# An encoder trunk on one core: three attentions of half B beside its q and k, and half B's last output projection two FFN steps earlier, in token sets of three and two with an FFN step behind every token tile

## The chip, the cores and the metric

The kernel runs on one core of a Trainium2 chip. The metric is the device time of one execution in microseconds (us); the time before is the median of three runs. Engines are called as the profile calls them: PE (TensorE matmul), PEld (its weight loads), DVE (VectorE), ACT (ScalarE), POOL (GpSimd), SP (SyncE, which issues most DMAs).

## The reference, cut to what matters

A trunk of two layers on 1024 prompt frames and 64 frames of a running stream, all in float32. Layer 0 mixes with RWKV-7 and gated linear attention, layer 1 with attention over a band of chunks; behind each mixing there is an output projection, a layer norm, a SwiGLU channel mixer (FFN) and another layer norm. The change touches layer 1:

```python
def chunk_band_attention(x, w_qkv, rel_table, w_o, cache_k, cache_v):
    qkv = (x @ w_qkv).reshape(Bsz, T, 3, C_HEADS, C_HEAD_DIM)
    q, k, v = (jnp.swapaxes(qkv[:, :, i], 1, 2) for i in range(3))
    o = ...          # softmax(q k / 8 + bias) v over a frame's own chunk and the 8 before it, 16 heads
    y = jnp.swapaxes(o, 1, 2).reshape(Bsz, T, D_MODEL) @ w_o
    return y, k_rows, v_rows
...
        x = layer_norm(DEEPNORM_ALPHA * x + mix, P['ln1_w'][layer], P['ln1_b'][layer])
        x = layer_norm(DEEPNORM_ALPHA * x + swiglu(x, P['ffn_w_in'][layer], P['ffn_w_out'][layer]),
                       P['ln2_w'][layer], P['ln2_b'][layer])
```

D_MODEL is 1024, there are 16 heads of 64, and the FFN's hidden width is 2816, which is 22 tiles of 128.

## The kernel before, in words

**Halves.** The tokens are split in half A (index 0: 384 prompt and the 64 sample frames, 448 columns) and half B (index 1: 640 prompt frames, five tiles of 128). The halves go through the same stages at different times, so that one half's vector work lies beside the other half's matmuls. Each float32 product is made of three fp32r products (high x high, low x high, high x low); a weight tile is loaded by `load_w` (L92) into one of two raw buffers `wr`, cast to `wh` on ACT (L101), and its rest `wl` is made on DVE (L106), on POOL (L108), or by both.

**The end of the program.** In `run`, half B's q and k are made for eight pairs of heads by `qk(1, hp)`; after the pairs listed in `self.AQ` (L1343) one attention of half B is queued there. An attention is queued in parts: score matmuls (L1283, L1284), softmax on DVE, ACT, DVE and POOL (L1287 to L1294), transposes on PE (L1299), casts on ACT and DVE (L1309, L1310), and the product with v (L1325, "PV"). Its result goes through DRAM (`og_d`). The other attentions lie in the loop at L1472 beside half A's FFN of layer 1, `f = self.ffn(0, 1, ...)` (L917), a generator of 22 steps: each `next(f)` is one step of 48 matmuls of 448 columns (L124 to L126), and behind the steps in GROUPS (16, 18 and 22 among them) comes a group of the second FFN matrix through `tsg` (L135 to L138 with `hh`, `hl`). When the loop at L1476 has done step `self.JM`, half B's last output projection is set up: its operand is loaded from `og_d` and cast (`load_xt`, L205 to L216, `yraw`), the residual x is loaded from `x_d` (`load_acc`, L797), one more `next(f)` runs, and `proj` (L851) goes through the token tiles in the order 2, 0, 3, 1, 4, in sets of which each loads all of `w_o`. `tsg` (L801) multiplies a tile (`part`, 12 matmuls of 512 columns), adds it to `acc` (L827), and behind a tile's last part calls `between` (another piece of `f`) and `after` (the layer norm).

**The layer norm** (L869) is a chain across three engines: L883 and L885 on DVE, L887 and L888 on POOL (`rstd`), L891 on DVE, then for the left half L893 on ACT and L894 on POOL and for the right half L896 on DVE, then eight transposes on PE (L901).

**Behind it** half B's last FFN runs as `s_ffn` (L1049), in products of fewer matmuls that need sums of the normed tokens (`chunk`, L966 to L1011, whose low halves L114 are put by POOL: eight `put` for each tile) and sums of the weights (`s_weights`, L1020: loads L1028, casts L1034 and L1035, four sums on POOL, L1040 to L1045). Half A's last layer norm `ln2` lies beside its first steps. The scheduler of the framework decides the order on each engine from the order in which the work is written and what each piece waits for.

Of the kernel before, what the change touches and what calls it, by code (L numbers as in the profile page):

```python
# [83 lines left out]
class Kern:  # L84
# [715 lines left out]
    def tsg(self, hf, acc, wsrc, pairs, hi, lo, first, after=None, packed=None, between=None, toks=None):  # L800

        def load(nh):
            ws = []
            for pr in pairs:
                h_, l_ = self.load_w(wsrc(nh, pr), [128, 2, 512])
                ws += [(h_[:, j, :], l_[:, j, :]) for j in range(2)]  # L810
            return ws

        kts = [2 * pr + j for pr in pairs for j in range(2)]
        toks = toks or self.toks(hf)

        def part(ws, nh, i, t0, m):
            two = packed and m == 64
            ps = self.bank()
            if two:
                self.gemm_ts(ps, ws, packed, None, kts, lambda x: x[:, 0:128])  # L820
            else:
                self.gemm_ts(ps[:m], ws, hi, lo, kts, lambda x: x[:, t0 : t0 + m])
            a = acc[i][:m, 512 * nh : 512 * nh + 512]
            if first:
                self.V.scalar_tensor_tensor(a, a, ALPHA, ps[:m], op0=ALU.mult, op1=ALU.add)
            else:
                self.V.tensor_tensor(a, a, ps[:m], op=ALU.add)  # L827
            if two:
                self.V.tensor_tensor(a, a, ps[m:], op=ALU.add)

        if after is None or between:
            for nh in range(2):
                ws = load(nh)
                for i, t0, m in toks:
                    part(ws, nh, i, t0, m)
                    if after and nh:
                        if between is not True:
                            between(i)
                        after(i)
        else:  # L840
            ws = [load(nh) for nh in range(2)]
            for i, t0, m in toks:
                for nh in range(2):
                    part(ws[nh], nh, i, t0, m)
                after(i)
# [491 lines left out]
    def run(self):  # L1337
# [2 lines left out]
        self.wkv_d = self.dp.tile([4, 128, 64], F32, name="wkv_d", tag="wkv_d")  # L1340
        self.gla_d = self.dp.tile([2, 128, 128], F32, name="gla_d", tag="gla_d")
        self.JX = 2
        self.PB, self.QB, self.turn, self.AQ = 1, 2, 0, (2, 5)  # L1343
        self.HB, self.PRE, self.JO, self.JM = 5, 4, 16, 18
        es_scan, es_one, es_ps = ExitStack(), ExitStack(), ExitStack()
        self.sp_ps = es_ps.enter_context(tc.tile_pool(name="scps", bufs=1, space=PS))
        self.tpsum = lambda: self.sbank("tps")
# [75 lines left out]
        with tc.tile_pool(name="qp", bufs=1) as qp:  # L1423
            self.vproj(0, qp, 2)
            for hp in range(4):
                if hp == self.JX:
                    with tc.tile_pool(name="yr1", bufs=1, side="right") as yp:
                        self.load_xt(1, self.yg_d, (4, 5, 6, 7, 0, 1, 2, 3), pool=yp)
                    acc1 = self.load_acc(1, a["x"], accp)
# [12 lines left out]
        f = self.ffn(1, 0, acc1, hp, lambda: self.layer_norm(1, acc1, "ln2", 0, xd(1)))  # L1442
# [11 lines left out]
        with tc.tile_pool(name="at1", bufs=1, side="right") as atp:  # L1454
# [16 lines left out]
            f = self.ffn(0, 1, acc0, hp, lambda: later.append, True)  # L1471
# [5 lines left out]
        for j in f:  # L1477
            if j == self.JM:
                self.gp2 = self.ctx.enter_context(tc.tile_pool(name="gp2", bufs=1, space=PS))
                self.tpsum = self.bank  # L1480
                accp = self.ctx.enter_context(tc.tile_pool(name="accB1", bufs=1, side="right"))
                self.xt[1] = self.xt_tiles(xbp, 1)
                with tc.tile_pool(name="yr2", bufs=1, side="right") as yp, tc.issue_after(self.last_w):
                    self.load_xt(1, self.og_d, pool=yp)
                    self.paired = True
                    acc1 = self.load_acc(1, self.x_d, accp)
                xs, sums = self.s_operands(self.ctx.enter_context(tc.tile_pool(name="sx", bufs=1, side="right")),
                                           self.ctx.enter_context(tc.tile_pool(name="st", bufs=1, side="right")))
                next(f)
                self.proj(1, acc1, "w_o", self.layer_norm(1, acc1, "ln1", 1, sums=sums), between=lambda i: next(f) if i in (3, 1, 4) else None, first=2)  # L1490
        es_a.close()
        hp = self.ctx.enter_context(tc.tile_pool(name="hpB1", bufs=1))
        outB = lambda t0, m: a["y_p"][PA + t0 : PA + t0 + m, :]
# [95 lines left out]
```

## Time and profile before

| | |
|---|---|
| median of 3 runs | 3117.12 us (3116.71 to 3119.89) |
| the profiled execution's own time | 3121.6 us |
| its span, first to last instruction | 3119.8 us |
| PE busy | 3017.0 us, 97% of the span |
| DVE, ACT, POOL busy | 2021.3, 1272.0, 1363.5 us |
| mean granted TensorE clock | 0.975 |

The page gives for each engine how long it was busy; the views below it give, for a stretch of the program, what an engine waited for. Times in the timeline count from the span's start. A matmul's own time there is longer than the distance from its start to the next one's, since matmuls overlap; costs are counted from start to start. The granted clock is 1.00 at 2.4 GHz and 0.50 at 1.2 GHz, the two levels that it has.

### The profile page before, as it was taken

The numbers are of one execution on the slowest core, as the hardware profiler recorded it, in microseconds if no ns is written. First come the engines' busy times: TensorE is split into PE (matmuls) and PEld (weight loads), VectorE is DVE, ScalarE is ACT, GpSimd is POOL, SyncE is SP. The second block draws the span as 40 slices with busy tenths as digits, with TensorE's granted clock in tenths as the row PEclk, the third lists the DMA queues.
The fourth block names the chain that finished last, engine by engine and source line by source line (L and its number), as shares of the span: only waits on it lengthen the run. The fifth ranks groups of instructions, "written<-read, shape, count | busy, mean of one in ns | idle before, by whom it ended". The sixth has DMA issues, their size and how long they took to land. (4 is left out here: it accounts for less than half of the span.)

```text
span 3119.8 us, 50045 instructions
## 1 busy us (share of the span) xinstructions
PE 3017.0 (97%) x17468; PEld 2676.2 (86%) x17468; DVE 2021.3 (65%) x4941; ACT 1272.0 (41%) x2761; POOL 1363.5 (44%) x1489
## 2 busy tenths in 40 slices
PE   9999999899999999999999999999999989899998
PEld 7788888688888887888999899899999978799987
DVE  4677875879898764455554466245666667766567
ACT  4454554344454323233443132345444433333332
POOL 2354534444454333443332233244555555745444
PEclk9989999889999999999999999999999999999999
DMA  6554334533533228444343232866455443322222
GB/s 201 140 155 119 108 109 123 141 105 109 137 110 112 89 97 274 140 134 123 116 133 105 81 95 98 247 201 182 126 150 145 132 160 107 116 80 95 67 82 75
DMA packets 298492, 399.29 MB, mean 128 GB/s; under 512 B 125504, under 2 KB 218552, under 8 KB 298240
## 3 DMA queue, kind: packets, MB, share of 16 engines
q1 hardware_dynamic: 297088, 393.48, 42.4%
q8 instruction: 138, 2.26, 0.3%
q10 hardware_dynamic: 1152, 2.62, 0.2%
q14 instruction: 114, 0.93, 0.1%
HBM read 323.63 MB, written 75.51 MB: 128 GB/s over the span
## 5 line engine op out<-in xcount | busy, mean ns | idle before, releaser
L108 POOL TENSOR_TENSOR wl<-wr,wh 128x512 fp32r<-128x512 f32 (+2 forms) x297 | 521.7, 1760 | 642.1 <-ACT wh L101 592.3
L124 PE MATMUL gps<-xh,wh 128*128 128x320 f32 (+1 forms) x2188 | 746.0, 341 | 7.8 <-ACT xh L215 5.9
L125 PE MATMUL gps<-xl,wh 128*128 128x320 f32 (+1 forms) x2188 | 745.0, 340 | 0.6 <-DVE xl L216 0.6
L126 PE MATMUL gps<-xh,wl 128*128 128x320 f32 (+1 forms) x2188 | 744.3, 340 | 0.9 <-DVE wl L106 0.9
L101 ACT CAST wh<-wr 128x1024 fp32r<-128x1024 f32 x360 | 375.8, 1048 | 457.3 <-PE gps L125 131.2
L106 DVE TENSOR_TENSOR wl<-wr,wh 128x512 fp32r<-128x512 f32 (+2 forms) x297 | 289.6, 975 | 248.9 <-ACT wh L101 246.0
L124 PEld LDWEIGHTS gps<-xh,wh 128*128 128x128 f32 x2188 | 414.4, 189 | 30.6 <-ACT xh L215 5.9
L126 PEld LDWEIGHTS gps<-xh,wl 128*128 128x128 f32 x2188 | 413.8, 189 | 19.9 <-DVE wl L106 2.1
L125 PEld LDWEIGHTS gps<-xl,wh 128*128 128x128 f32 x2188 | 414.0, 189 | 18.1 <-DVE xl L216 1.0
L1294 POOL TENSOR_SCALAR s<-s,mx 128x640 f32<-128x640 f32 (+5 forms) x144 | 203.9, 1416 | 272.1 <-DVE mx L1293 250.7
L135 PE MATMUL gps<-wh,xh 128*128 128x512 f32 x661 | 262.0, 403 | 6.8 <-ACT xh L1092 2.5
L138 PE MATMUL gps<-wh,xl 128*128 128x512 f32 x661 | 258.9, 399 | 6.1 <-DVE xl L216 6.1
L136 PE MATMUL gps<-wl,xh 128*128 128x512 f32 x661 | 263.0, 400 | 1.3 <-DVE wl L106 1.1
L136 PE MATMUL gps<-wl,hh 128*128 128x512 f32 x572 | 226.7, 398 | 0.3 <-DVE wl L106 0.3
L135 PE MATMUL gps<-wh,hh 128*128 128x512 f32 x572 | 226.2, 397 | 0.3 <-DVE acc L827 0.3
L827 DVE TENSOR_TENSOR acc<-acc,gps 128x512 f32<-128x512 f32 x216 | 143.6, 679 | 86.8 <-PE gps L138 83.6
L138 PE MATMUL gps<-wh,hl 128*128 128x512 f32 x484 | 189.5, 398 | 2.2 <-DVE hl L942 2.2
L549 DVE TENSOR_TENSOR t<-lt,x 16x48 f32<-16x48 f32 (+9 forms) x540 | 147.3, 273 | 35.8 <-DMA lt<-l_d 25.4
L1292 ACT ACTIVATE s<-s,mx 128x640 f32<-128x640 f32 (+5 forms) x144 | 96.4, 669 | 162.3 <-DVE mx L1291 153.8
L135 PEld LDWEIGHTS gps<-wh,xh 128*128 128x128 f32 x661 | 125.9, 191 | 37.6 <-ACT wh L101 4.3
L138 PEld LDWEIGHTS gps<-wh,xl 128*128 128x128 f32 x661 | 125.7, 190 | 34.4 <-DVE xl L216 6.9
L136 PEld LDWEIGHTS gps<-wl,xh 128*128 128x128 f32 x661 | 126.2, 191 | 30.4 <-DVE wl L106 2.7
(383 smaller groups left out, 6327.8 us busy)
## 6 DMA issues: line engine op xcount, KB each, us to landing
wr<-in_w_fi SPq DMA_DIRECT2D x176, 512.0 KB
wr<-in_w_fo SPq DMA_DIRECT2D x88, 512.0 KB
wr<-in_w_in SPq DMA_DIRECT2D x44, 512.0 KB
wr<-in_w_qk SPq DMA_DIRECT2D x32, 512.0 KB
wr<-in_w_o SPq DMA_DIRECT2D x24, 512.0 KB
qs<-qd SPq DMA_DIRECT2D x32, 320.0 KB
wr<-in_w_om SPq DMA_DIRECT2D x16, 512.0 KB
wr<-in_w_v SPq DMA_DIRECT2D x16, 512.0 KB
```

Source lines behind the costliest of these rows:

```text
L101: self.A.copy(hi, raw)
L106: self.V.tensor_tensor(lo[:, :h], raw[:, :h], hi[:, :h].bitcast(F32), op=ALU.subtract)
L108: self.G.tensor_tensor(lo[:, h:], raw[:, h:], hi[:, h:].bitcast(F32), op=ALU.subtract)
L124: self.T.matmul(ps, hi[:, kt, :], xh, start=(kt == 0), stop=False)
L125: self.T.matmul(ps, hi[:, kt, :], xl, start=False, stop=False)
L126: self.T.matmul(ps, lo[:, kt, :], xh, start=False, stop=(kt == nk - 1))
L135: self.T.matmul(ps, xh, wh, start=(i == 0), stop=False)
L136: self.T.matmul(ps, xh, wl, start=False, stop=(lo is None and i == n - 1))
L138: self.T.matmul(ps, cols(lo(kt)), wh, start=False, stop=(i == n - 1))
L549: V.tensor_tensor(tv, lt[:, j, w:16].unsqueeze(2).to_broadcast([m, r, w]), x[:, 0, j, 0:w].unsqueeze(1).to_broadcast([m, r, w]), op=ALU.mult)
L827: self.V.tensor_tensor(a, a, ps[:m], op=ALU.add)
L1294: G.tensor_scalar(s[:m, :nk], s[:m, :nk], mx[:m, 3:4], None, op0=ALU.mult)
```

## The change

Four edits, with no change in what is computed:

- `AQ` is (1, 3, 5) instead of (2, 5): three attentions of half B lie beside its q and k, and five instead of six beside half A's FFN (the loop at L1472 starts at `len(self.AQ)`, with two steps of `f` to each attention).
- `JM` is 16 instead of 18: the projection is set up behind step 16, and step 17 (with the second matrix's group 16 to 18) runs ahead of its first matmul.
- `first=3`: the token sets are 2, 0, 3 and 1, 4 instead of 2, 0 and 3, 1, 4. `w_o` is loaded twice as before.
- `between` runs a step of `f` behind every token tile, where before only behind tiles 3, 1 and 4. For the last tile of a set `tsg` calls the norm first and the step behind it.

```diff
@@ tsg @@
                     part(ws, nh, i, t0, m)
                     if after and nh:
-                        if between is not True:
-                            between(i)
-                        after(i)
+                        if between is True:
+                            after(i)
+                            continue
+
+                        fs = (between, after)
+                        for f in fs if i != toks[-1][0] or not self.paired else fs[::-1]:
+                            f(i)
@@ run @@
-        self.PB, self.QB, self.turn, self.AQ = 1, 2, 0, (2, 5)
-        self.HB, self.PRE, self.JO, self.JM = 5, 4, 16, 18
+        self.PB, self.QB, self.turn, self.AQ = 1, 2, 0, (1, 3, 5)
+        self.HB, self.PRE, self.JO, self.JM = 5, 4, 16, 16
@@ run, the projection @@
                 next(f)
-                self.proj(1, acc1, "w_o", self.layer_norm(1, acc1, "ln1", 1, sums=sums), between=lambda i: next(f) if i in (3, 1, 4) else None, first=2)
+                self.proj(1, acc1, "w_o", self.layer_norm(1, acc1, "ln1", 1, sums=sums), between=lambda i: next(f), first=3)
```

Line numbers behind L842 are four higher in the kernel after (L901 becomes L905, L1040 becomes L1044).

**PE at the norm of tile 2.** Before, the last matmul of tile 2's part, the first four transposes of its norm, and the next part (tile 0):

```order
L136 MATMUL gps_28091<-wl_28087,xh1_27815 128x512
L138 MATMUL gps_28091<-wh_28086,xl1_27816 128x512
L901 MATMUL gps_28123<-ident_71,acc_27852 128x128 x4
L135 MATMUL gps_28136<-wh_28079,xh1_27815 128x512
L136 MATMUL gps_28136<-wl_28080,xh1_27815 128x512
```

And now, with step 18 of half A's FFN (48 matmuls, the first, and the last two) between:

```order
L138 MATMUL gps_27987<-wh_27982,xl1_27594 128x512
L124 MATMUL gps_28015<-xh0_69,wh_28003 128x448
...
L125 MATMUL gps_28043<-xl0_70,wh_28010 128x448
L126 MATMUL gps_28043<-xh0_69,wl_28011 128x448
L905 MATMUL gps_28085<-ident_71,acc_27630 128x128 x4
L905 MATMUL gps_28092<-ident_71,acc_27630 128x128 x4
L135 MATMUL gps_28105<-wh_27975,xh1_27593 128x512
```

Before, nothing stood between tile 2's last matmul and its transposes; now a whole step does.

**PE at the norm of tile 3, the last of the first set.** Now, its last matmul, the first tile of set 2 (12 matmuls, `gps_28404`), the transposes, and then step 20:

```order
L138 MATMUL gps_28241<-wh_27982,xl1_27594 128x512
L135 MATMUL gps_28404<-wh_28378,xh1_27593 128x512
...
L138 MATMUL gps_28404<-wh_28385,xl1_27594 128x512
L905 MATMUL gps_28266<-ident_71,acc_27634 128x128 x4
L905 MATMUL gps_28273<-ident_71,acc_27634 128x128 x4
L124 MATMUL gps_28317<-xh0_69,wh_28305 128x448
```

Before, tile 3 had a step between its last matmul and its transposes; now 12 matmuls of 512 columns stand there, and the step stands behind.

**POOL around the first weights of half B's last FFN.** Before, from the norm of tile 4 (L887 to L894) on; L1040 to L1045 are the four sums of one step's weights, L114 the eight puts of tile 4's sums:

```order
L887 TENSOR_SCALAR rstd<-mv 128x1
L888 TENSOR_TENSOR rstd<-rstd,mhalf 128x1
L894 TENSOR_TENSOR acc<-acc,gb 128x512
L1040 TENSOR_TENSOR wr<-wr 128x512
L1041 TENSOR_TENSOR wr<-wr 128x512
L1043 TENSOR_TENSOR wr<-wr 128x512
L1045 TENSOR_TENSOR wr<-wr 128x512
L114 TENSOR_TENSOR xl_27816<-ss,xh_27815 128x4x64
L114 TENSOR_TENSOR S3l<-sc,S3h 128x4x64
L114 TENSOR_TENSOR S2l<-su,S2h 128x4x64
L1040 TENSOR_TENSOR wr<-wr 128x512
L114 TENSOR_TENSOR S4l<-ss,S4h 128x4x64
```

And now (L1044 to L1049 are those four sums, L891, L892 and L898 the norm's instructions, here of half A's `ln2` from the second group on):

```order
L114 TENSOR_TENSOR S4l<-ss,S4h 128x4x64
L114 TENSOR_TENSOR xl_27594<-ss,xh_27593 128x4x64
L114 TENSOR_TENSOR S3l<-sc,S3h 128x4x64
L114 TENSOR_TENSOR S2l<-su,S2h 128x4x64
L114 TENSOR_TENSOR S4l<-ss,S4h 128x4x64
L1044 TENSOR_TENSOR wr<-wr 128x512
L891 TENSOR_SCALAR rstd<-mv 128x1 x2
L1045 TENSOR_TENSOR wr<-wr 128x512
L892 TENSOR_TENSOR rstd<-rstd,mhalf 128x1 x2
L1047 TENSOR_TENSOR wr<-wr 128x512
L898 TENSOR_TENSOR acc<-acc,gb 128x512 x2
L1049 TENSOR_TENSOR wr<-wr 128x512
```

The first step's four sums stood ahead of tile 4's eight puts; now they stand behind them, with pieces of half A's norm between.

**PE where the attentions pass from q and k to half A's FFN.** Before, a score tile of the first attention beside the FFN (`sps_24014`), the matmuls behind it, and its transposes (`tp_24026`); left out are 35 FFN matmuls of 448 columns, another tile's transposes and scores:

```order
L1284 MATMUL sps_24014<-ks_23963,qs_23964 128x320
L1325 MATMUL op_23652<-pl_21823,vt_23361 128x128
L1179 MATMUL tps_23944<-ident_71,qf_23935 128x128
...
L1299 MATMUL tp_23984<-ident_71,s_23977 128x128 x4
L126 MATMUL gps_24310<-xh0_69,wl_24278 128x448
...
L1284 MATMUL sps_24053<-ks_23963,qs_23964 128x320
...
L124 MATMUL gps_24355<-xh0_69,wh_24343 128x448
L1299 MATMUL tp_24026<-ident_71,s_24019 128x128 x4
```

And now, the same for the score tile `sps_23937`, whose softmax is `s_23942`; left out are 10 more matmuls of that PV (L1329) and the other scores of `sps_24282` and `sps_24299`:

```order
L1288 MATMUL sps_23937<-ks_23824,qs_23825 128x320
L1329 MATMUL op_23898<-ph_21822,vt_23669 128x384
L1329 MATMUL op_23898<-pl_21823,vt_23669 128x384
...
L1287 MATMUL sps_24282<-ks_24271,qs_24272 128x512
...
L1303 MATMUL tp_23926<-ident_71,s_23919 128x128 x4
L1303 MATMUL tp_23933<-ident_71,s_23919 128x128
L1287 MATMUL sps_24299<-ks_24271,qs_24272 128x320
...
L1288 MATMUL sps_24299<-ks_24271,qs_24272 128x320
L1303 MATMUL tp_23949<-ident_71,s_23942 128x128 x4
```

Before, the FFN's matmuls stand between a tile's scores and its transposes; now one PV, two other score tiles and one other tile's transposes.

## Rows read from the trace of the kernel before

**Rows 1.** The page's first part, of the whole span: busy time, share and instructions of each engine.

```profile
PE 3017.0 (97%) x17468; PEld 2676.2 (86%) x17468; DVE 2021.3 (65%) x4941; ACT 1272.0 (41%) x2761; POOL 1363.5 (44%) x1489
```

**Rows 2.** The view of waits, PE, 2490 to 2760 us: what PE waited for, us in total, times, the longest.

```profile
PE gps L901 <- DVE acc L896: 9.3, 1, 9.3
PE gps L1062 <- ACT xh L113: 7.4, 1, 7.4
PE gps L1062 <- ACT wh L1034: 4.4, 4, 2.8
PE gps L135 <- ACT wh L101: 2.1, 1, 2.1
PE gps L138 <- DVE xl L216: 1.2, 1, 1.2
PE gps L135 <- ACT xh L215: 1.0, 1, 1.0
```

**Rows 3.** The view by windows, of three stretches: the last attentions beside the FFN, the projection around its first norm, the first steps of half B's last FFN. Columns: the stretch and its length in us, busy us and instructions of PE, PEld, DVE, ACT and POOL, granted clock, share of the DMA engines, GB/s.

```profile
2184.00:2496.00 312.00, 312.00 (x1728) 283.28 (x1727) 194.84 (x451) 147.41 (x283) 160.27 (x123) 1.00 0.48 138
2568.00:2600.00 32.00, 24.20 (x104) 19.82 (x105) 23.03 (x39) 11.26 (x20) 18.65 (x16) 0.84 0.31 96
2658.00:2690.00 32.00, 23.30 (x141) 21.84 (x138) 29.79 (x47) 12.10 (x24) 24.37 (x21) 0.84 0.22 76
```

**Rows 4.** The timeline around the start of the projection (start us, us, engine, line, operation, what it writes and reads; in brackets the idle time ahead of it and what ended it): two matmuls of the FFN step ahead of it, the second and the last of 30, and the projection's first.

```profile
2532.66 0.36 PE L125 MATMUL gps<-xl,wh 128*128 128x448 f32 x1
...
2538.34 0.37 PE L126 MATMUL gps<-xh,wl 128*128 128x448 f32 x1
2539.68 0.50 PE L135 MATMUL gps<-wh,xh 128*128 128x512 f32 x1 [0.98 <-ACT xh L215]
```

**Rows 5.** The timeline of ACT there: the last five of the eight casts of the projection's operand.

```profile
2542.67 4.00 ACT L215 CAST xh<-yraw 128x640 fp32r<-128x640 f32 x5 [0.37 <-DMA yraw<-og_d]
```

**Rows 6.** The timeline of PE from tile 2's last matmul to its transposes and on: matmuls of 512 columns, and the transposes (L901).

```profile
2566.10 0.40 PE L138 MATMUL gps<-wh,xl 128*128 128x512 f32 x1
2575.80 1.12 PE L901 MATMUL gps<-ident,acc 128*128 128x128 f32 x4 [9.30 <-DVE acc L896]
...
2577.14 0.63 PE L136 MATMUL gps<-wl,xh 128*128 128x512 f32 x1
...
2579.27 0.63 PE L135 MATMUL gps<-wh,xh 128*128 128x512 f32 x1
```

**Rows 7.** The timeline, all engines, for tile 0: its last sum on DVE, and its transposes.

```profile
2581.24 0.68 DVE L827 TENSOR_TENSOR acc<-acc,gps 128x512 f32<-128x512 f32 x1
...
2589.84 1.04 PE L901 MATMUL gps<-ident,acc 128*128 128x128 f32 x8
```

**Rows 8.** The timeline of POOL from 2651 to 2691 us: the first step's first and last weight sum (four in all), the first, the second and the last of the eight puts, the last weight sum of the second step, and half A's last norm.

```profile
2651.23 1.68 POOL L1040 TENSOR_TENSOR wr<-wr 128x512 f32<-128x512 f32 x1 [2.36 <-DVE wl L1035]
...
2655.72 1.29 POOL L1045 TENSOR_TENSOR wr<-wr 128x512 f32<-128x512 f32 x1
2662.81 0.86 POOL L114 TENSOR_TENSOR xl<-ss,xh 128x256 fp32r<-128x256 f32 x1 [5.79 <-ACT xh L113]
2664.59 1.61 POOL L114 TENSOR_TENSOR S3l<-sc,S3h 128x256 fp32r<-128x256 f32 x1 [0.92 <-ACT S3h L113]
...
2674.61 0.73 POOL L114 TENSOR_TENSOR S4l<-ss,S4h 128x256 fp32r<-128x256 f32 x1
2675.30 1.29 POOL L1045 TENSOR_TENSOR wr<-wr 128x512 f32<-128x512 f32 x1
2676.67 1.38 POOL L887 TENSOR_SCALAR rstd<-mv 128x1 f32<-128x1 f32 x2
2678.14 1.53 POOL L888 TENSOR_TENSOR rstd<-rstd,mhalf 128x1 f32<-128x1 f32 x2
2679.64 3.16 POOL L894 TENSOR_TENSOR acc<-acc,gb 128x512 f32<-128x512 f32 x2
2684.28 2.78 POOL L887 TENSOR_SCALAR rstd<-mv 128x1 f32<-128x1 f32 x1 [1.49 <-DVE mv L885]
```

**Rows 9.** The timeline of PE ahead of tile 4's transposes (17 matmuls of 512 columns from the first of these rows to the second), and of DVE: the last cast of the weights of steps 2 and 3 of half B's last FFN.

```profile
2653.78 0.39 PE L135 MATMUL gps<-wh,hh 128*128 128x512 f32 x1
...
2657.40 0.39 PE L136 MATMUL gps<-wl,hh 128*128 128x512 f32 x1
2657.63 1.03 PE L901 MATMUL gps<-ident,acc 128*128 128x128 f32 x8
...
2705.54 1.21 DVE L1035 TENSOR_TENSOR wl<-wr,wh 128x1024 fp32r<-128x1024 f32 x1
...
2720.86 1.21 DVE L1035 TENSOR_TENSOR wl<-wr,wh 128x1024 fp32r<-128x1024 f32 x1
```

**Rows 10.** The timeline of one softmax of an attention beside half A's FFN: the first and the last of its five pieces.

```profile
2186.79 0.82 DVE L1287 CUSTOM_DVE_ANT_0 s<-sps,bias 128x640 f32<-128x640 f32 x1 [0.28 <-PE sps L1284]
...
2189.67 1.89 POOL L1294 TENSOR_SCALAR s<-s,mx 128x640 f32<-128x640 f32 x1 [2.81 <-DVE mx L1293]
```

**Rows 11.** The view of waits, PE, 2028 to 2184 us (the end of half B's q and k, with an attention beside it).

```profile
PE tps L1179 <- ACT qf L1162: 0.8, 2, 0.4
PE tp L1299 <- DVE o L1330: 0.7, 1, 0.7
PE op L1325 <- DVE pl L1310: 0.6, 2, 0.3
```

## The prediction, as it went on record

> **What bounds the kernel now.** I read the page first, to see which engine sets the time; then the waits of PE, to see which idle stretches are left; then the windows and the timeline around each. PE is busy 97% of the span [rows 1], so the number of matmuls, which the change leaves alone, sets almost all of the time, and a change of order can move only PE's waits and the stretches at the lower clock. Between 2490 and 2760 us three places stand out [rows 2]. At the start of half B's projection PE waits 1.0 and 1.2 us for the operand and 2.1 us for a cast of weights. At the norm of tile 2 it waits 9.3 us. At the start of half B's last FFN it waits 7.4 us for tile 4's sums, and 4.4 us in four pieces for weights. Behind the two long waits the granted clock is low, 0.84 over a window of 32 us each, where the stretch of the attentions is at 1.00 and wholly busy [rows 3]. So there are about 25 us to be had here, and next to none in the stretch ahead of it.
>
> The sum is made against the profiled execution's 3121.6 us (span 3119.8), which is 4.5 us over the median of 3117.12; I scale the result by their ratio at the end. A measurement of this kernel can tell about 0.2% from no change, 6.2 us, so "faster" means under 3110.9 and "slower" over 3123.4.
>
> **The change part by part.** Two prices recur. A step of half A's FFN is 48 matmuls that start 0.203 us apart (28 intervals from 2532.66 to 2538.34, [rows 4]), 9.7 us. A token tile's part is 12 matmuls at 0.226 us (16 intervals from 2653.78 to 2657.40, [rows 9]), 2.7 us.
>
> *Start of the projection, JM 16.* The five casts that end the operand begin at 2542.67 and last 4.0 us [rows 5], while the projection's first matmul is at 2539.68 and the FFN matmul before it at 2538.34 [rows 4]: the load follows the last attention by 30 matmuls only. Now 12 more matmuls of step 16, the 48 of step 17 and 44 of the second FFN matrix stand between, some 22 us. The waits 1.0, 1.2, 2.1 and two of 0.2 go, 4.7 us, with 1.6 us for the eight matmuls behind them at half clock (an estimate, 8 times the 0.2 us that [rows 6] show between the two distances). I leave 1.0 for a residue, since twelve loads now meet the loads of FFN weights: **-5.4** (bounds -6.4 and 0).
>
> *Norm of tile 2.* Its chain takes from the last matmul at 2566.10 to the transposes at 2575.80, 9.3 us of it idle; then matmuls start 0.43 us apart (five from 2577.14 to 2579.27), not 0.23 [rows 6], which over some ten costs 2.0. Step 18 now lies between, 9.7 us for a chain of 9.3. Tile 0 shows the chain at 8.6 us from L827 to the transposes, with other work beside it and no wait in the list [rows 2, 7]. So **-11.3** (bounds -11.3 and -9).
>
> *Norm of tile 3.* This is the price of calling the norm ahead of the step for a set's last tile. Where a whole step covered it, 12 matmuls of set 2 do: 9.3 less 2.7 is 6.6 us idle, and 2.0 at the low clock: **+8.6** (bounds: the 8.6 us chain of tile 0 less 2.7 without clock loss, +5.9; and with DVE also busy for the FFN, +11). The scheduler could have put more of set 2 there, but the order says it did not: those matmuls wait for a weight slot that tile 3's own part frees.
>
> *Start of half B's last FFN.* Tile 4's norm now comes ahead of most of the last group, so 56 matmuls of 512 columns, 12.7 us, follow its transposes and cover the sums for which PE waited 7.4 us. But POOL's order changes too. Before, the first step's four weight sums ran from 2651.23 to 2657.0, ahead of the puts; now they stand behind all eight and among half A's norm. Counted from the start of tile 4's transposes (2657.63 before, [rows 9]): the first put comes 5.2 us later (2662.81), eight puts of 0.7 to 1.6 take some 8, four sums 5.8, two rstd 1.4, two powers 1.5, two additions 3.2 [rows 8], and the last cast 1.2 [rows 9]: the first step's weights are whole at +26.3, or +27.4 with a wait of ACT for its cast. Later steps follow at 15.3 us (2705.54 to 2720.86, [rows 9]), so step 3's are at +73.3; before, they were at 2722.07, +64.4. That is 8.9 later, counted from transposes that stand earlier: 32 matmuls behind tile 4's part, not 74, is -9.5, and a norm chain of 9.3 behind 7.2 us of matmuls adds a wait of 2.1. Fourteen more matmuls of the last group lie behind tile 4's part, so 3.2 us of work is saved ahead of it. Together 8.9 - 9.5 + 2.1 - 3.2 = **-1.7**. The wait for sums becomes a wait for weights. Bounds: -9.2 if weights never bind (7.4 and 1.8 of clock), +10 if POOL is slower (below).
>
> *Set 2 with two tiles.* A pair of w_o tiles now feeds two parts instead of three, so weights must come faster for 2.7 us each; the same pair rate in set 1 before cost a few tenths [rows 2]: **+1.0** (0 to +3).
>
> *Third attention beside q and k.* Two attentions there left waits of 0.8, 0.7 and 0.6 [rows 11], so one more adds 1.0. At the passage to the FFN three score tiles have only 3.2 to 3.8 us of PE work before their transposes, while a softmax takes from 2186.79 to 2191.56, 4.8 us [rows 10]: 1.0 to 1.6 us each, some 3.4, and a fourth with 4.3 adds 0.8: **+5.2**. Bounds: 0, since the attentions beside the FFN left none [rows 3], and +8 if five tiles fall short. One attention less beside the FFN saves nothing, as PE was wholly busy there.
>
> Sum: -5.4 - 11.3 + 8.6 - 1.7 + 1.0 + 5.2 = -3.6, so 3118.0 for the profiled execution and **3113.5** in terms of the median: within the 6.2 us.
>
> **The rivals.**
>
> *Weights do not bind (faster).* If POOL's sums of weights slip between the puts while DVE makes the next ones (POOL sat idle 0.9 us between the first two, [rows 8]), the whole 9.2 us at the start of the last FFN is won, 7.5 more than forecast: **3106**. For it: before, PE waited for weights only in pieces of up to 2.8 [rows 2]. Against it: POOL executes in the order written, and that puts the sums last.
>
> *POOL held up beside DVE (slower).* POOL's tiny L887 takes 0.7 us in one place and 2.78 in another, where DVE works on two operands in SBUF back to back [rows 8]. Now such L887 stand among the first two steps' weight sums. Four of them at 2.8 instead of 0.7 add 8.4, and eight puts and sums at 1.7 instead of 1.3 another 3.2. It decides as soon as PE waits for weights, because then each us is passed on one to one: 11.6 more, **3125**. Against it: other L887 stayed at 0.7 beside the same DVE lines. The Trainium skill, page "SBUF — State Buffer", section "SBUF: two separate sides", says that the port pair of VectorE and GpSimd is an exclusive lock, taken also by a VectorE instruction with two SBUF inputs against a GpSimd one that reads SBUF, and that the loser blocks fully. The 2.78 us [rows 8] agrees in kind. A lock held for one instruction alone would give less than that at each, and by it this rival's time would lie between the forecast and 3125.
>
> *The third attention is free (faster).* If the passage costs nothing, since softmaxes overlap other tiles' products, the sum is 5.2 lower: **3108**. For it: 312 us without a wait [rows 3]. Against it: there 35 FFN matmuls lay between a score tile and its transposes, where now a PV lies.
>
> That the change does not do what it says is partly so: tile 3 gets no step behind it in time, which is in the sum.
>
> **How the numbers follow.** Forecast 0.39 (its own range 3107 to 3120; 0.08 of it lies under 3110.9, 0.01 over 3123.4), weights free 0.27, POOL held up 0.22 (0.03 of it within the 6.2 us), third attention free 0.12 (0.07 under the bound). Faster: 0.08 + 0.27 + 0.07 = 0.42. Slower: 0.01 + 0.19 = 0.20. Same: 0.38. The range goes from 3101, weights free with the third attention's cost half gone, to 3126 for the slow rival.
>
> **What would show it.** Right: the waits for the operand's casts and the 9.3 us at tile 2 are gone; a wait of 6 to 8 us for L900 (L896 before) stands at tile 3's transposes; at the start of the last FFN PE waits for casts of weights (L1038) by 6 to 10 us instead of for xh; some tenths to 1.5 us at L1303 around the passage from q and k to the FFN. Wrong: no wait at tile 3, or none for weights, or over 15 us for them, or a wait that is in no list here, such as tile 0's or tile 1's norm behind a step.

## The result: slower by half a per cent, and the profile after

The changed kernel takes 3130.68 us in the median of 7 runs (3124.65 to 3139.24), the kernel before on the same chips 3116.71. The ratio is 1.0047, 95% interval [1.0037, 1.0058]: 11.5 to 18.1 us slower, 14.7 in the middle. The forecast was 3113.5, no measurable change, with a range up to 3126 and a chance of 0.20 for slower. The time lies above the range.

One profile cannot place 14.7 us by its span alone: in the profiles of this study the last matmul ahead of the changed stretch, which is the same work in all, stands anywhere between 1988.4 and 1998.1 us. So times below are medians of runs on one chip, given as ratios, and the trace is read for where a wait stands. The changed kernel was not timed beside the experiments, so a difference to it is less sure than one interval says. The profiled execution of the changed kernel is near its median, 3130.19 us with a span of 3128.4. PE is busy as long as before [rows 1], in a longer span:

```profile
PE 3014.1 (96%) x17468; PEld 2677.2 (86%) x17468; DVE 2018.5 (65%) x4941; ACT 1272.4 (41%) x2761; POOL 1364.9 (44%) x1489
```

The waits of PE at the end of q and k and the passage to half A's FFN (2000 to 2490 us; the kernel before has no others there than those of [rows 11]):

```profile
PE sps L1287 <- DMA ks<-kd: 3.3, 1, 3.3
PE tps L1183 <- ACT qf L1166: 2.2, 3, 1.5
PE tp L1303 <- POOL s L1298: 1.3, 2, 0.7
PE op L1329 <- DVE pl L1314: 1.3, 3, 0.6
PE sps L1287 <- DVE mx L1291: 1.2, 2, 0.9
PE op L1329 <- ACT ph L1313: 0.8, 1, 0.8
```

And the longest from the projection into half B's last FFN (2490 to 2830 us), against [rows 2], which end at 2760:

```profile
PE gps L1066 <- ACT wh L1038: 13.7, 5, 6.3
PE gps L135 <- ACT xh L113: 3.2, 1, 3.2
PE gps L1068 <- DVE wl L1039: 2.3, 2, 1.7
PE gps L135 <- DVE acc L827: 2.3, 1, 2.3
PE gps L135 <- DVE ht L940: 1.9, 1, 1.9
PE gps L905 <- POOL acc L898: 1.6, 1, 1.6
```

What was to go has gone: the operand's casts (L215, L216), the 9.3 us at tile 2's norm, the 7.4 us for tile 4's sums. What came is 10.1 us in the first list, where 2.1 stood, and in the second list three things: waits for the first weights, 13.7 and 2.3 us, where 6.5 and 0.3 stood up to 2830 (up to 2760, 11.7 where 4.4 stood); a wait of 3.2 us of the second matrix's matmuls (L135), put down to a cast of xh, which stood in no forecast; and tile 3.

Tile 3's norm, in the timeline of PE, with one row of DVE and one of PEld (bracketed: the idle time and what ended it):

```profile
2586.78 0.67 DVE L827 TENSOR_TENSOR acc<-acc,gps 128x512 f32<-128x512 f32 x1
...
2587.57 0.19 PEld L135 LDWEIGHTS gps<-wh,xh 128*128 128x128 f32 x1 [2.73 <-issue]
2587.60 0.47 PE L135 MATMUL gps<-wh,xh 128*128 128x512 f32 x1 [2.32 <-DVE acc L827]
...
2590.86 0.80 PE L136 MATMUL gps<-wl,xh 128*128 128x512 f32 x1 [0.92 <-DVE wl L106]
...
2594.93 1.97 PE L905 MATMUL gps<-ident,acc 128*128 128x128 f32 x8 [1.57 <-POOL acc L898]
```

The 12 matmuls of set 2 are broken by waits of 2.3 and 0.9 us for a free bank (the PSUM buffer in which a part is summed, and which is free again when DVE has added it to `acc`, L827) and for their weights, and the transposes stand 1.6 us behind them: 4.8 us idle, and the transposes come 9.7 us behind the end of tile 3's last matmul, the same chain as tile 2's 9.3 us [rows 6]. The window around it has the granted clock of [rows 3], which loses 5.1 of its 32 us:

```profile
2568.00:2600.00 32.00, 27.18 (x122) 22.58 (x121) 26.10 (x48) 13.96 (x29) 18.10 (x17) 0.84 0.27 97
```

The new wait of 3.2 us, all engines: tile 4's last matmul, then ACT and DVE, and the matmul that waits with its weight load (PEld):

```profile
2638.26 0.40 PE L138 MATMUL gps<-wh,xl 128*128 128x512 f32 x1
...
2639.39 1.04 ACT L101 CAST wh<-wr 128x1024 fp32r<-128x1024 f32 x1 [2.46 <-DMA wr<-in_w_fo]
...
2640.47 0.69 DVE L106 TENSOR_TENSOR wl<-wr,wh 128x512 fp32r<-128x512 f32 x1 [1.45 <-ACT wh L101]
...
2641.08 0.68 DVE L827 TENSOR_TENSOR acc<-acc,gps 128x512 f32<-128x512 f32 x1
...
2641.52 0.37 ACT L113 CAST xh<-gps 128x256 fp32r<-128x256 f32 x1
...
2641.87 0.19 PEld L135 LDWEIGHTS gps<-wh,hh 128*128 128x128 f32 x1 [3.66 <-ACT S4h L113]
2641.90 0.47 PE L135 MATMUL gps<-wh,hh 128*128 128x512 f32 x1 [3.25 <-ACT xh L113]
```

The profile infers who ended a wait, and here the rows speak against the cast of xh that it names: the matmul's weight load starts at 2641.87, before that cast ends at 2641.89. What ended 0.11 us ahead of the weight load is DVE's L827, which adds tile 4's part to `acc`; at tile 3, where the profile itself names L827, the distance is 0.12 (2587.45 to 2587.57). It is 0.11 or 0.12 in the five experiments that have this wait too (E1, E3, E4, E7, E12). The matmul reads hh and wh and nothing that L827 makes, so what it waited for is most likely its output bank, which tile 4's own part held until then. L827 was late because DVE, in order, had first stood 1.45 us for a cast of weights (L106 for L101), for which ACT had stood 2.46 us for a load of the second matrix.

The start of tile 4's transposes on PE, and POOL from the last of tile 4's puts on, against [rows 8, 9]:

```profile
2650.89 1.04 PE L905 MATMUL gps<-ident,acc 128*128 128x128 f32 x8
```
```profile
2661.92 0.74 POOL L114 TENSOR_TENSOR S4l<-ss,S4h 128x256 fp32r<-128x256 f32 x1 [0.80 <-ACT S4h L113]
2665.59 1.68 POOL L1044 TENSOR_TENSOR wr<-wr 128x512 f32<-128x512 f32 x1 [2.93 <-DVE wl L1039]
2667.35 3.07 POOL L891 TENSOR_SCALAR rstd<-mv 128x1 f32<-128x1 f32 x2
2670.50 1.26 POOL L1045 TENSOR_TENSOR wr<-wr 128x512 f32<-128x512 f32 x1
2671.72 1.06 POOL L892 TENSOR_TENSOR rstd<-rstd,mhalf 128x1 f32<-128x1 f32 x2
2672.76 2.29 POOL L1047 TENSOR_TENSOR wr<-wr 128x512 f32<-128x512 f32 x1
2675.01 3.51 POOL L898 TENSOR_TENSOR acc<-acc,gb 128x512 f32<-128x512 f32 x2
2678.48 1.28 POOL L1049 TENSOR_TENSOR wr<-wr 128x512 f32<-128x512 f32 x1
```

The first step's four sums (L1044, L1045, L1047, L1049), 5.8 us before, take 14.2 from 2665.59 to 2679.76 with the pieces of half A's norm between them, and start only when DVE has cast the first weights, 2.9 us behind the last put. They are done 28.9 us behind the start of the transposes. PE's first long wait for weights, 6.3 us, ends at 2676.18 with the cast of what the third sum made (L1038, 2675.08 to 2676.13), its next, 0.6 us, at 2680.89 with the cast behind the fourth.

### The profile page after: what moved, and what is told of

The parts are those of the page before. It is cut to its first block, busy times and chain, and to the rows that moved or that the text cites. A ratio compares the mean times of both kernels' runs of the same rounds, so it can differ in the third digit from the quotient of the medians.

```text
span 3128.4 us, 50069 instructions
## 1 busy us (share of the span) xinstructions
PE 3014.1 (96%) x17468; PEld 2677.2 (86%) x17468; DVE 2018.5 (65%) x4941; ACT 1272.4 (41%) x2761; POOL 1364.9 (44%) x1489
## 4 chain that ended last, share of the span: by engine, by line
PE 77%; DVE 7%; DMA 7%; POOL 3%; issue 3%; ACT 2%; SPq 1%; POOLq 0%; DVEq 0%; ACTq 0%
PE gps L124 11%; PE gps L125 11%; PE gps L126 11%; PE gps L135 7%; PE gps L136 7%; PE gps L138 7%; PE gps L1066 2%; PE gps L1068 2%; PE gps L1067 2%; PE op L1329 2%; PE tp L1303 2%; POOL wl L108 1%; PE sps L1287 1%; PE ps L622 1%; PE sps L1288 1%
## 5 line engine op out<-in xcount | busy, mean ns | idle before, releaser
L101 ACT CAST wh<-wr 128x1024 fp32r<-128x1024 f32 x360 | 375.4, 1048 | 476.9 <-PE gps L125 138.7
L106 DVE TENSOR_TENSOR wl<-wr,wh 128x512 fp32r<-128x512 f32 (+2 forms) x297 | 287.6, 969 | 252.5 <-ACT wh L101 250.4
L135 PE MATMUL gps<-wh,xh 128*128 128x512 f32 x661 | 259.4, 400 | 5.3 <-ACT xh L1096 2.5
L135 PE MATMUL gps<-wh,hh 128*128 128x512 f32 x572 | 228.0, 400 | 5.4 <-ACT xh L113 3.2
L827 DVE TENSOR_TENSOR acc<-acc,gps 128x512 f32<-128x512 f32 x216 | 143.3, 678 | 84.4 <-PE gps L138 79.3
L135 PEld LDWEIGHTS gps<-wh,xh 128*128 128x128 f32 x661 | 125.2, 190 | 35.4 <-issue 3.4
```

Source lines behind the costliest of these rows:

```text
L101: self.A.copy(hi, raw)
L106: self.V.tensor_tensor(lo[:, :h], raw[:, :h], hi[:, :h].bitcast(F32), op=ALU.subtract)
L135: self.T.matmul(ps, xh, wh, start=(i == 0), stop=False)
```

## The experiments

Each was timed in five rounds beside the kernel before on the same chip; a per cent is 31.2 us.

**E1 and E2: the attentions.** AQ back in the changed kernel, and AQ alone in the kernel before:

```diff
E1  -        self.PB, self.QB, self.turn, self.AQ = 1, 2, 0, (1, 3, 5)
E1  +        self.PB, self.QB, self.turn, self.AQ = 1, 2, 0, (2, 5)
E2  -        self.PB, self.QB, self.turn, self.AQ = 1, 2, 0, (2, 5)
E2  +        self.PB, self.QB, self.turn, self.AQ = 1, 2, 0, (1, 3, 5)
```

E1: 

> The changed kernel with AQ back at (2, 5). Theory A (the attentions beside q and k cost it): the waits of PE between 2000 and 2190 us, 10.1 us in the changed kernel, fall to the 2.0 us of the kernel before, with one stretch of 3.4 us at half clock less; that is 9.8 us less than the changed kernel's median, about +5 us against the kernel before. Rival B (the loss is at the norms and weights of the projection and of half B's last FFN; waits at q and k are given back later): within 3 us of the changed kernel, +12 to +18 us against the kernel before.

Measured 1.0065 [1.0051, 1.0079], 20 us slower than before and, with intervals that overlap, 6 slower than the changed kernel: both theories missed. The waits at q and k fell as A said, but others came beside the last attention (PE, 2498 to 2516 us), and there the clock fell too (2498 to 2522 us, columns as in [rows 3]; 1.00 in the kernel before):

```profile
PE sps L1287 <- DVE mx L1291: 2.5, 2, 1.3
PE gps L124 <- DVE o L1334: 0.9, 1, 0.9
PE op L1329 <- ACT xh L1313: 0.9, 2, 0.6
PE op L1329 <- DVE xl L1314: 0.7, 2, 0.4
```
```profile
2498.00:2522.00 24.00, 18.38 (x75) 15.05 (x74) 8.40 (x24) 7.41 (x18) 7.50 (x4) 0.72 0.09 28
```

That is 5.6 us of waits, with two short ones more, and 6.7 us of clock, over the 9.8 that A expected to save. Six attentions beside the FFN with the projection set up behind step 16 leave two steps fewer behind the last one than either kernel has. AQ and JM hang together: the third attention at q and k pays for the earlier projection.

E2: 

> The kernel before with AQ at (1, 3, 5) alone. Theory A: +8 to +11 us against the kernel before, with a wait of PE of about 3 us for the load of ks at the first attention's first scores and about 5 us in small waits where the attentions pass to half A's FFN. Rival B: within 3 us of the kernel before, since later waits shrink by what is lost here. Two FFN steps more stand behind the attentions here, so the start of the projection is as before.

Measured 1.0033 [1.0022, 1.0044], +10.3 us: A holds. The list has the same kinds of waits as the changed kernel's (1.7 for ks, where A had 3, 2.2 for qf, 1.3, 1.3, 1.2, 0.5). In this trace the clock fell at the passage, where it is 1.00 in the changed kernel (2164 to 2184 us):

```profile
2162.00:2184.00 22.00, 17.63 (x94) 15.21 (x92) 9.84 (x31) 10.22 (x23) 11.44 (x9) 0.84 0.61 159
```

**E3 and E4: tile 3's norm.** The norm ahead of the step for tile 4 alone; E4 with AQ at (2, 5) too.

```diff
-                        for f in fs if i != toks[-1][0] or not self.paired else fs[::-1]:
+                        for f in fs if i != 4 or not self.paired else fs[::-1]:
```

E3: 

> The changed kernel with tile 3's step ahead of its norm again (the norm comes first for tile 4 alone). Theory C (tile 3's norm is not covered by 12 matmuls): the waits at tile 3, 4.8 us in three pieces, and most of a stretch of 10.2 us at half clock go, 7 to 9 us less than the changed kernel, +6 to +8 us against the kernel before. Rival D (half A's step 20, now earlier, only shifts what is late, and POOL and DVE are late for weights a little further on): within 3 us of the changed kernel.

Measured 1.0016 [1.0006, 1.0027], +5.0, 9.7 less than the changed kernel: C holds, and none of tile 3's three waits is left in the trace (PE is busy throughout from 2568 to 2620 us, at a clock of 1.00).

E4: 

> Both: AQ at (2, 5) and tile 3's step ahead of its norm. If A and C both hold and add: 17 to 19 us less than the changed kernel, that is -5 to -2 us against the kernel before, and no wait over 1 us between 2000 and 2190 us nor at tile 3. If only one holds, +4 to +8 us against the kernel before.

Measured 1.0031 [1.0019, 1.0044], +9.7. It misses, for E1's reason: AQ back costs 4.7 us here, 5.6 there.

**E5: which part of the attentions.** The kernel before with two attentions beside q and k, the first one pair earlier: `AQ = (1, 5)`.

> The kernel before with AQ at (1, 5): two attentions beside q and k as before, the first one pair of heads earlier, so that the passage to half A's FFN is as before. It parts the 11 us that three attentions there cost (from the first transpose of k to the end of half B's last FFN in the trace). Theory A1 (the load of ks is late whenever the first attention stands one pair behind its k): a wait for the load of 1.7 to 3.3 us and one stretch at half clock, +2 to +5 us against the kernel before, and no wait at the passage. Rival A2 (the load's wait comes from the third attention, or is given back): within 1.5 us of the kernel before, all 11 us being the passage's.

Measured 1.0022 [1.0012, 1.0032], +6.9: A1's mechanism, above its size. The other waits there come to 2.5 us, 2.1 in [rows 11]; the load has one, in the timeline of PE, and the window behind it is partly at the lower clock (columns as in [rows 3]):

```profile
2026.23 0.76 PE L1283 MATMUL sps<-ks,qs 128*128 128x512 f32 x1 [3.61 <-DMA ks<-kd]
```
```profile
2026.20:2036.40 10.20, 10.17 (x51) 9.96 (x52) 3.61 (x11) 2.75 (x7) 1.57 (x1) 0.71 0.71 256
```

The wait of 3.6 us and 10.2 us at a granted clock of 0.71, 3.0 lost, make 6.6 of the 6.9. By the medians some two thirds of AQ's 10.3 us would belong to the first attention, which stands one pair of heads behind the k that it loads back from DRAM, and the rest to the passage. The intervals leave this split open by 5 us either way, and the traces part it otherwise: this load costs 1.7 us in E2, with a clock of 1.00 behind it, and 3.3 us with 1.7 of clock in the changed kernel. Shown is that the first attention's place costs by itself, not its share.

**E6 and E9: tile 4's norm.** E6 has the step ahead of the norm for every tile (`for f in fs:`); E9 for tile 4, with tile 3's norm first as changed (`if i != 3`).

E6: 

> The changed kernel with the step ahead of the norm for every tile, tile 3 and tile 4 both; beside the run with tile 3's alone it tells what tile 4's early norm is worth. Theory E (the early norm only turns a wait for tile 4's sums into one for the first weights): the 6.3 us for weights at the start of half B's last FFN goes and the 7.4 us for the sums comes back; within 3 us of the run with tile 3's step alone, +2 to +8 us against the kernel before. Rival F (the early norm is worth the sums' wait): 7 to 10 us slower than that run, +12 to +15 us against the kernel before.

Measured 0.9989 [0.9979, 1.0000], -3.4: 8.4 us faster than E3, where theory E had allowed 3 and F expected a loss. The early norm of tile 4 is not worth nothing, it costs. In the trace of E6 the sums' wait is back and the 3.2 us for the bank are gone:

```profile
PE gps L1066 <- ACT wh L1038: 9.4, 5, 3.0
PE gps L1066 <- ACT xh L113: 7.4, 1, 7.4
PE gps L135 <- DVE ht L940: 2.9, 1, 2.9
```

E9: 

> The changed kernel with tile 4's step ahead of its norm and tile 3's norm first as changed: the other half of the pair. If the two norms' costs add (tile 3's norm first 9.7 us, tile 4's 8.4 us, from the runs with one and with both put back), +4 to +9 us against the kernel before, with no wait of the second matrix's first matmul for a cast of xh, the 7.4 us for sums at the start of half B's last FFN back, and the waits at tile 3 as in the changed kernel. Rival (they do not add, because what is late at tile 3 covers what is late at tile 4): +11 us or more.

Measured 1.0016 [1.0006, 1.0025], +5.0: the two norms' costs add. Tile 3's norm first costs 9.7 (the changed kernel against E3) and 8.4 (E9 against E6); tile 4's 9.7 (the changed kernel against E9) and 8.4 (E3 against E6). Each of these four differences is open by 4 to 5 us. The traces agree: at tile 3, idle time and lower clock come to 4.8 and 5.1 us in the changed kernel, 5.2 and 3.4 in E9, none in E3. From tile 4's last matmul to the last matmul at L1066 to L1068, the changed kernel takes 449.8 us and E3 450.8, E9 441.4 and E6 445.2, so that tile 4's norm first costs 8.4 and 5.6. Some 5 us of it are the wait for the bank and a stretch of 3.4 us at half clock behind it; the later weights are the likely rest.

**E7 and E10: half A's norm among the weights.** E3 and E6 with half A's last norm held back behind the weight sums of its step:

```diff
-        G.tensor_tensor(g[:, b2], g[:, b2], u[:, b2], op=ALU.subtract)
+        self.last_ws = G.tensor_tensor(g[:, b2], g[:, b2], u[:, b2], op=ALU.subtract).ins
...
-            with self.tc.issue_after(self.last_w), self.tc.issue_after(self.last_sum):
+            with self.tc.issue_after(self.last_ws), self.tc.issue_after(self.last_sum):
```

E7: 

> The changed kernel with tile 3's step ahead of its norm, and half A's last norm not to be issued before the weight sums of the same step of half B's last FFN (it then stands behind the second step's sums on POOL, where it stood among the first step's). Theory G (the pieces of that norm among the sums are what makes the first weights late): the first step's sums on POOL take 6 to 7 us instead of 14, the waits of PE for casts of weights there fall by 5 us or more, 4 to 8 us less than the run with tile 3's step alone, -3 to +1 us against the kernel before. Rival H (the first weights are late because DVE and ACT cast them behind tile 4's sums; POOL only follows): under 3 us less, +2 to +5 us against the kernel before.

Measured 0.9995 [0.9986, 1.0004], -1.6, 6.6 less than E3: G's time holds, its signs only in part. POOL's four sums now stand together, 8.3 us from first to last, where G had 6 to 7:

```profile
2654.89 1.68 POOL L1044 TENSOR_TENSOR wr<-wr 128x512 f32<-128x512 f32 x1 [2.93 <-DVE wl L1039]
2656.65 3.88 POOL L1045 TENSOR_TENSOR wr<-wr 128x512 f32<-128x512 f32 x1
2660.61 1.26 POOL L1047 TENSOR_TENSOR wr<-wr 128x512 f32<-128x512 f32 x1
2661.95 1.27 POOL L1049 TENSOR_TENSOR wr<-wr 128x512 f32<-128x512 f32 x1
```

One of them took 3.88 us beside DVE's work, and PE's first long wait for weights is 3.9 us, where E3 had 6.3. But all waits for casts of weights together (L1038 and L1039) fall by 2.0 us, from 14.9 to 12.9, where G had 5 or more. The clock gives some 1.7 more (0.85 in E3 over the 35 us from 2664, 0.90 in E7 over those from 2654); the rest of the 6.6 is not placed. DVE's cast of the first weights behind tile 4's sums, H's point, is still in it.

E10: 

> The changed kernel with the step ahead of the norm for every tile, and half A's last norm behind the weight sums of its step. If that norm's pieces cost in the first steps of half B's last FFN whatever waits first there, 3 to 7 us less than with the steps alone, -10 to -6 us against the kernel before. Rival (they cost only where the weights are awaited first, as behind tile 4's early norm): within 3 us of the run with the steps alone, -6 to 0 us against the kernel before.

Measured 1.0000 [0.9991, 1.0009]: no better than E6, 3.4 us above it. With the step ahead of tile 4's norm, the rival holds, at its edge: the norm's pieces cost only where the weights are awaited first.

**E8, E11 and E12: a cover for tile 2 that the attentions don't pay.** The kernel before with one step taken from ahead of the projection and put behind tile 2; E11 with E7's edit as well; E12 with tile 4's norm ahead of its step on top.

```diff
-        self.HB, self.PRE, self.JO, self.JM = 5, 4, 16, 18
+        self.HB, self.PRE, self.JO, self.JM = 5, 4, 16, 17
...
-                self.proj(1, acc1, "w_o", ..., between=lambda i: next(f) if i in (3, 1, 4) else None, first=2)
+                self.proj(1, acc1, "w_o", ..., between=lambda i: next(f) if i in (2, 3, 1, 4) else None, first=2)
```

E8: 

> The kernel before with JM at 17 and a step behind tiles 2, 3, 1 and 4, all else as before (AQ, sets of two and three, the step ahead of the norm): the cover for tile 2's norm without the attentions moved. Theory I (a step behind tile 2 is worth its 9.3 us wait and 2 us of clock when it is paid for by one step fewer ahead of the projection, not by the attentions): the 9.3 us wait goes, the waits at the start of the projection grow by 0 to 3 us, -11 to -7 us against the kernel before. Rival J (the step taken from ahead of the projection is missed there or beside the last attention just as much): within 4 us of the kernel before.

Measured 0.9983 [0.9975, 0.9992], -5.3, between the two theories. The 9.3 us are gone, but the waits of the projection are 7.5 us now, where 4.8 stood (4.3 of them in [rows 2]), with 2.3 more beside the last attention:

```profile
PE gps L124 <- ACT wh L101: 2.1, 1, 2.1
PE gps L135 <- ACT xh L215: 1.7, 1, 1.7
PE gps L136 <- DVE wl L106: 1.3, 2, 1.1
PE gps L135 <- ACT wh L101: 1.3, 1, 1.3
PE gps L901 <- POOL acc L894: 1.1, 1, 1.1
```

E11: 

> The kernel before with JM at 17, a step also behind tile 2, and half A's last norm behind the weight sums of its step; attentions, sets and the order of step and norm as before. If the two add: -11 to -7 us against the kernel before, with no wait over 2.5 us at tile 2, and waits for casts of weights at the start of half B's last FFN of under 5 us where the run without the last edit had 8.7. Rival (the norm's pieces only move): -7 to -3 us.

Measured 0.9991 [0.9982, 1.0001], -2.8: as in E10 the edit gains nothing behind a late norm; the rival's end, if anything. The waits for casts of weights are 7.5 us, not under 5.

E12: 

> As the run before it, and tile 4's norm ahead of its step. With the first weights made early, tile 4's early norm could be worth the 7.4 us for the sums that it was meant to take away: -16 to -10 us against the kernel before. Rival (the early norm brings a wait for a PSUM bank of 3 us, one stretch at half clock, and a wait for the first weights, and is worth nothing again): -8 to -2 us, that is no better than the run before it.

Measured 0.9976 [0.9967, 0.9986], -7.5: faster than both kernels, 4.4 to 10.3 us under the kernel before, which is itself under the changed one. The time is at the rival's end, and its reasons are there: the wait for the bank, 3.3 us, and the waits for weights. Its conclusion is not: with the early norm the time is 4.7 us below E11, with intervals that just overlap. E8, 2.2 us above E12, is not told apart from it.

```profile
PE gps L1066 <- ACT wh L1038: 8.9, 6, 3.8
PE gps L135 <- ACT xh L113: 3.3, 1, 3.3
PE gps L1068 <- DVE wl L1039: 2.3, 3, 0.9
```

## Why the prediction was wrong

Put together, the changed kernel is: attentions +10.3 (E2), tile 3's norm +8.4 to +9.7, tile 4's norm +8.4 to +9.7, and all the rest -13.7 (E6's -3.4 less E2's +10.3). With 9 for each norm that is +14.6, against 14.7 measured. This sum is no test: its terms are differences along one chain of runs that begins and ends with the same two kernels. The test is that each norm costs about the same with and without the other (E9).

*Start of the projection and norm of tile 2* (-5.4, -11.3, and +1.0 for set 2, -15.7 together): about right. The rest of the sum above is -13.7, open by 5 us, and holds whatever else parts E6 from E2. The waits named are gone. Missing from the sum was the 1.9 us ahead of the second matrix's group, which now stands right behind step 17: it ends with DVE's L940, which reads step 17's product (2523.93), behind 5.6 us that DVE spent on three low halves of the projection's operand (L216).

*Norm of tile 3* (+8.6): right in mechanism and size, 8.4 to 9.7, though not in its parts: its idle time is split in three, 4.8 us in all where 6.6 was forecast, and the lower clock takes 5.1 where 2.0 was.

*Third attention* (+5.2): the step that failed by a term left out. The passage was seen: 4.7 us in six waits in the trace, 4.2 forecast for it. What I did not look for is where the moved attention starts. I counted the work between a tile's scores and its transposes, and not the loads ahead of its first scores. With its first attention at pair 1 instead of 2, the load of ks, which has to wait for k to be written to DRAM (in the waits of SyncE, 2010 to 2030 us), is late by 3.3 us, and the 3.6 us behind it have a granted clock of 0.53. These 5.0 us are what the term lacks against E2's +10.3; E5, with the first attention alone moved, gives +6.9.

```profile
SPq L1261 <- DMA kd<-qh: 5.6, 1, 5.6
```

*Start of half B's last FFN* (-1.7): the step that failed most. It was right that the sums' wait turns into one for the first weights. Of the 6 to 10 us named for it, the longest piece has 6.3, and all pieces up to 2760 us have 11.7. But the sum took 32 matmuls behind tile 4's part as cover that begins at once. They waited 3.2 us, most likely for the bank that tile 4's own part still held: DVE, which empties it, stood for a cast of weights, and ACT, which makes that cast, for a load. I followed the chain of the norm, and not who frees the next matmul's bank. With 3.4 us at half clock behind that, the transposes came 12.2 us behind the end of tile 4's last matmul, where the sum had 9.3. And POOL's first sums were done 28.9 us behind the start of the transposes, where the terms gave 25.1: they began behind a DVE cast that I took as free, and took 14.2 us with the norm's pieces where I had 11.9. These 2.9 and 3.8 us turn -1.7 into +5.0. By the runs it came out at +8.4 to +9.7, by the traces at 5.6 and 8.4, so up to some 4 us stay open.

*The rivals.* "POOL held up beside DVE" forecast 3125 for another reason than the one that decided: the first pair of L891 lasted 3.07 us together, not 2.8 each, and its 8.4 us are not there; slower instructions make 2.3 us of the first sums' 14.2. What cost there is the place of half A's pieces among the sums, 6.6 us by E7. One weight sum of 3.88 us in E7, beside others of 1.26, is a POOL instruction held up of the kind that the rival had in mind; DVE ran four L895 beside it, each with two operands in SBUF. The Trainium skill, page "SBUF — State Buffer", section "SBUF: two separate sides", would put that down to the lock on the shared port pair, and no run here parts this from other causes. "Weights do not bind" is refuted by the waits for weights, "the third attention is free" by E2.

## What to carry to other kernels

When work is moved earlier, look at what its first instruction loads and how long ago that was written, not only at what stands around its middle. An early consumer (here a norm ahead of the step that covered it) is worth its wait only if everything else that its successor needs is early too: the weights, a free bank, and the engine that empties it. And two edits may be one: two steps fewer ahead of the projection were only affordable with one attention fewer beside them, so undoing one edit alone made it worse, while one step fewer (E8) paid without it. Last, a profile's name for what ended a wait is worth a look at the rows: a cast that ends after the waiting engine has started did not release it.

## What the runs showed that was not expected

A short wait can cost nearly twice itself: in E5 the wait of 3.6 us for ks was followed by 10.2 us at a mean granted clock of 0.71, with PE busy throughout. In E2 a wait of 1.7 us in the same place was followed by a clock of 1.00. Nor does the same run of waits always cost the same: at the passage, waits of up to 1.5 us each went with a clock of 0.84 over 22 us in E2 and of 1.00 in the changed kernel. And the same POOL sum of 128x512 took from 1.26 to 3.88 us in E7 alone, by what DVE did beside it.
